# A store at the end of a mixture-of-experts kernel: expert 5's rows divided over two queues

## The chip, the cores and the metric

The kernel runs on one core of a Trainium2 chip. The metric is the device time of one execution in microseconds (us); lower is better. A profile of one execution stands beside the times; its span runs from the first to the last instruction and is a little shorter than the execution's time.

## The reference

Eight experts, each with its own 256 rows of x, its own two weight matrices and biases; everything is float32.

```python
n_experts, capacity, hidden, expert_hidden = 8, 256, 512, 2048

def reference(x, w1, w2, b1, b2):
    h = np.matmul(x, w1) + b1[:, np.newaxis, :]
    h = np.maximum(h, 0)
    return (np.matmul(h, w2) + b2[:, np.newaxis, :]).astype(np.float32)
```

x is 8 x 256 x 512, w1 is 8 x 512 x 2048, w2 is 8 x 2048 x 512, and the output is 8 x 256 x 512. The weights are 64 MB in all, and each is used once.

## The kernel before

**Loads.** Nearly everything is moved by DMAs that GpSimd issues, because these turn float32 in memory into fp16 in SBUF on the way. `load_x`, `load_w1` and `load_w2` fetch one expert each: x in 128 partitions of 2 rows, w1 in 128 partitions of 4 rows of the hidden dimension, w2 in 128 partitions of 16 rows. `load_w2_piece` (its DMA is L91) fetches the last expert's w2 in eight pieces: (0, 4), (4, 7), (7, 10) and (10, 12) of the 16 rows with all 512 columns, then (12, 14) and (14, 16) with the first 320 columns, and both again with the other 192. Only the first two experts' x (by SyncE and ScalarE, as float32) and b1 (by ScalarE) take another way in.

**Products.** For each expert `first_product` makes 16 tiles of h (128 x 256), each of four matmuls (L113); ScalarE adds the bias, applies relu and writes fp16 (L120). `second_product` starts each accumulator with a one-row matmul that adds b2 (L163), then adds up 16 matmuls of 128 x 512 for each of two row halves (L175). For expert 7 the accumulators are split by columns, 320 and 192, to follow the pieces of its w2. The outer loop runs 11 stages: stage s makes the first product of expert s (while there is one) and the second product of expert s - 3.

**Stores.** `store` copies the two accumulators out of PSUM, one by VectorE (L138) and one by ScalarE (L139), into one SBUF tile of 128 partitions x 1024 float32. Each partition is one row of 4 KB in the store: two rows of the output that lie next to each other. For experts 0 to 6 it only notes the store in `pending`; the DMA is issued later by `flush` (L132), on GpSimd. Expert 7's stores go out at once: the 320 columns by SyncE (L149), the 192 columns half by SyncE (L142) and half by ScalarE (L143).

**The ring.** All of GpSimd's DMAs from expert 1 on stand in a list written out by hand, `ring`. Each entry has a stage from which it may be issued, and entries are issued strictly in the list's order; `ordered` keeps that order in the program. In the steady part a stage brings x and w1 of the next expert, w2 of the expert three back, and the store of the expert before that. At the end of the list stand the eight pieces of expert 7's w2, with the store of expert 4 after the first piece. The stores of the experts in `LATE`, 5 and 6, stand behind the last piece, in that order:

```python
    for e in LATE:
        ring.append((e + LAG + 1, flush, (e,)))
```

The waits on GpSimd's DMAs come from data, from free buffers, and from completion counts: the DMAs take turns on eight completion semaphores, so each one waits until the DMA eight places before it in GpSimd's order has landed. For expert 5's store the one eight places before is expert 4's store. For expert 6's store it is the piece (4, 7) of expert 7's w2.

SyncE issues only three DMAs: the first expert's x at the start, and expert 7's two stores (L149, L142) at the end.

Of the kernel before, what the change touches and what calls it, by code (L numbers as in the profile page):

```python
# [11 lines left out]
def kernel(  # L12
# [9 lines left out]
    nc = tc.nc  # L22
    fp32 = mybir.dt.float32
    fp16 = mybir.dt.float16
    E, T, H = x.shape
    M = w1.shape[2]
    P = 128
# [3 lines left out]
    HL = 320  # L31
    LAG = 3
    LATE = (5, 6)
    RING = (0, 1, 2, 3, 4) + LATE
    PARTS = {}
    nXF32 = 2

    def ordered(ins):
        return tc.keep_in_program_order(ins)
# [89 lines left out]

    def flush(e):  # L130
        dst, src = pending.pop(e)
        ordered(nc.gpsimd.dma_start(out=dst, in_=src))  # L132

    def store(e, po, c0, c1, split):
        w = c1 - c0
        pool = out_pool if w == H else singles
        out_sb = pool.tile([P, nTB, w], fp32, tag=f"out{c0}_{w}", name=f"out{w}")
        nc.vector.tensor_copy(out=out_sb[:, 0, :], in_=po[0])  # L138
        nc.scalar.copy(out=out_sb[:, 1, :], in_=po[1])  # L139
        dst = out[e].rearrange("(p tb) h -> p tb h", tb=nTB)[:, :, c0:c1]  # L140
        if split and c1 == H:
            nc.sync.dma_start(out=dst[:, 0, :], in_=out_sb[:, 0, :])  # L142
            nc.scalar.dma_start(out=dst[:, 1, :], in_=out_sb[:, 1, :])  # L143
        elif e in RING:
            pending[e] = (dst, out_sb)
        else:
            step = P // PARTS.get(e, 1)
            for lo in range(0, P, step):
                nc.sync.dma_start(out=dst[lo : lo + step], in_=out_sb[lo : lo + step])  # L149

    def second_product(e):
        if e < E - 1:
# [17 lines left out]
        for lo, hi, p0, p1, t in w2_sb[e]:  # L170
            mine = [b for b in blocks if p0 <= b[0] and b[1] <= p1]
            for tb in range(nTB):
                for j in range(lo, hi):
                    for c0, c1, _, _ in mine:
                        ordered(nc.tensor.matmul(  # L175
                            out=acc[c0, tb],
                            lhsT=hT[e][:, j, tb * P : (tb + 1) * P],
                            rhs=t[:, j - lo, c0 - p0 : c1 - p0],
                            start=False,
                            stop=(j == nJ - 1),  # L180
                        ))
            if hi == nJ:
                for c0, c1, _, _ in mine:
                    store(e, [acc[c0, tb] for tb in range(nTB)], c0, c1, e == E - 1)

    x32 = singles.tile([P, nXF32, nTB, H], fp32)
    for e in range(nXF32):
# [4 lines left out]
        out=b2_sb,  # L192
        in_=b2.rearrange("e h -> (e h)").rearrange("(o f) -> o f", o=1),
# [10 lines left out]
    for j in range(nJ):  # L204
        for s in range(2):
            ordered(nc.tensor.matmul(  # L206
                out=pb[s * 64 : (s + 1) * 64, j, :, :],
# [5 lines left out]
    for s in range(2):  # L213
        nc.vector.tensor_copy(  # L214
            out=b1T[s * 64 : (s + 1) * 64, :, :], in_=pb[s * 64 : (s + 1) * 64, :, :, s]
# [6 lines left out]
    for s in range(1, E + LAG - 1):  # L222
        if s < E:
            if s >= nXF32:
                ring.append((s - 2, load_x, (s,)))
            ring.append((s - 2, load_w1, (s,)))
        if s >= LAG:
            ring.append((s - 2, load_w2, (s - LAG,)))
        if s >= 2 * LAG:
            ring.append((s - 2, flush, (s - 2 * LAG,)))  # L230
    e = E - LAG - 1
    for piece in (
        (0, 4, 0, H), (4, 7, 0, H), (7, 10, 0, H), (10, 12, 0, H),
        (12, 14, 0, HL), (14, 16, 0, HL), (12, 14, HL, H), (14, 16, HL, H),
    ):
        ring.append((0, load_w2_piece, (E - 1,) + piece))
        if e in RING and e not in LATE:
            ring.append((e + LAG + 1, flush, (e,)))
            e += 1
    for e in LATE:  # L240
        ring.append((e + LAG + 1, flush, (e,)))
# [40 lines left out]
```

## Time and profile before

| what | value |
|---|---|
| time, median of 4 runs | 183.57 us (183.33 to 183.68) |
| time of the profiled execution | 183.33 us |
| its span | 181.6 us |
| PE busy | 138.1 us (76% of the span) |
| ScalarE busy | 62.7 us (35%) |
| GpSimd busy | 22.1 us (12%) |
| VectorE busy | 13.4 us (7%) |
| time of GpSimd's DMA packets, share of 16 engines | 97.9% |
| read from and written to memory | 71.39 MB and 4.19 MB |

PE is the name of TensorE's matmuls, PEld of its weight loads, DVE of VectorE, ACT of ScalarE, POOL of GpSimd and SP of SyncE. The sixteen DMA engines serve the queues of GpSimd (q0), SyncE (q1), ScalarE (q10) and the fetches of instructions (q8, q14). Busy time is summed for each engine; the engines run beside each other. A DMA that an engine issues shows as a short instruction on that engine's line, and the time from issue to landing is listed apart; a DMA posts one completion count from each of the sixteen engines, and has landed with the last of them. Line numbers (L132) are those of the kernel before.

### The profile page before, as it was taken

What the parts mean: (1) busy time and instruction counts of PE and PEld (TensorE: products, weight loads), DVE (VectorE), ACT (ScalarE), POOL (GpSimd) and SP (SyncE); (2) the same over time, 40 slices, a digit from 0 to 9 for tenths busy, and PEclk for the clock granted to TensorE, in tenths of its full rate; (3) what the DMA queues carried; (4) which work ended last, traced back from release to release, by engine and by line L of the source; (5) the groups of instructions that cost most, each with busy time, mean ns of one, the idle gap of its engine ahead of it and who ended that gap; (6) DMA issues with size and microseconds to landing.
All of it is one profiled execution on the core that took longest, in us unless ns stands there. A gap on an engine that the chain in (4) does not pass through costs nothing.

```text
span 181.6 us, 2204 instructions
## 1 busy us (share of the span) xinstructions
PE 138.1 (76%) x946; PEld 98.4 (54%) x946; DVE 13.4 (7%) x22; ACT 62.7 (35%) x138; POOL 22.1 (12%) x46
## 2 busy tenths in 40 slices
PE   0555999489640999649995999409999995999990
PEld 0544889369540946547464747308559641334670
DVE  0320011001000101010000110001010010100010
ACT  0022679548560422705136604503309501010100
POOL 7100020300300011010110002000004003113300
PEclk9999999969995699965999999965999999699999
DMA  5989998999999999999999999999999999999995
GB/s 186 283 180 233 231 220 184 209 253 213 193 231 231 206 199 231 198 236 202 231 227 184 224 231 224 184 285 213 199 224 222 280 199 273 211 245 281 215 283 186
DMA packets 7017, 40.58 MB, mean 224 GB/s; under 512 B 1216, under 2 KB 2256, under 8 KB 4960
## 3 DMA queue, kind: packets, MB, share of 16 engines
q0 software_dynamic: 5872, 38.81, 97.9%
q1 hardware_dynamic: 688, 0.95, 1.6%
q10 hardware_dynamic: 448, 0.69, 1.0%
q8 instruction: 7, 0.11, 0.2%
q14 instruction: 2, 0.02, 0.0%
HBM read 71.39 MB, written 4.19 MB: 416 GB/s over the span
## 4 chain that ended last, share of the span: by engine, by line
DMA 60%; PE 25%; issue 8%; another core or an unknown queue 2%; POOL 2%; ACT 0%; POOLq 0%
DMA x<-in_x_dram 24%; DMA w2sb<-in_w_dram 23%; PE acc L175 17%; DMA w1sb<-in_w_dram 13%; PE ph L113 7%; PE acc L163 1%; PE psx L100 1%; POOL w2sb L85 1%; POOL w1sb L75 1%; POOL out_dram L132 0%; POOL b_sb L191 0%; POOL ident masks.py:199 0%; POOL ident masks.py:197 0%; ACT out L139 0%
## 5 line engine op out<-in xcount | busy, mean ns | idle before, releaser
L113 PE MATMUL ph<-xT,w1sb 128*128 128x256 f16 x512 | 67.8, 299 | 8.7 <-DMA w1sb<-in_w_dram 8.7
L120 ACT ACTIVATE hT<-ph,b1T 128x256 f16<-128x256 f32 x128 | 56.9, 474 | 43.6 <-PE ph L113 43.5
L113 PEld LDWEIGHTS <-w1sb 128*128 128x128 f16 x512 | 61.4, 149 | 14.4 <-DMA w1sb<-in_w_dram 9.6
L175 PE MATMUL acc<-w2sb,hT 128*128 128x512 f16 x224 | 51.2, 388 | 2.1 <-DMA w2sb<-in_w_dram 2.1
L175 PEld LDWEIGHTS <-hT 128*128 128x128 f16 x288 | 27.5, 99 | 32.8 <-issue 7.4
L139 ACT COPY out<-acc 128x512 f32<-128x512 f32 (+2 forms) x9 | 4.9, 541 | 60.0 <-PE acc L175 60.0
L100 PE MATMUL psx<-ident,x 128*128 128x128 f16 x64 | 6.6, 265 | 21.5 <-DMA x<-in_x_dram 20.8
L100 PEld LDWEIGHTS <-x 128*128 128x128 f16 x64 | 5.3, 128 | 22.5 <-DMA x<-in_x_dram 21.7
L75 POOL DMA_DIRECT2D w1sb<-in_w_dram x8 | 4.4, 553 | 61.7 <-PE ph L113 60.9
L106 DVE COPY xT<-psx 128x1024 f16<-128x1024 f16 x8 | 5.5, 692 | 83.0 <-PE psx L100 83.0
L138 DVE COPY out<-acc 128x512 f32<-128x512 f32 (+2 forms) x9 | 5.7, 632 | 72.1 <-PE acc L175 72.1
L85 POOL DMA_DIRECT2D w2sb<-in_w_dram x8 | 4.3, 536 | 48.9 <-PE acc L175 48.9
L206 PE MATMUL pb<-ident,b_rows 16*64 16x16 f32 x64 | 3.7, 265 | 6.7 <-DMA b_rows<-in_b_dram 6.7
L175 PE MATMUL acc<-w,hT 128*128 128x320 f16 (+1 forms) x64 | 7.4, 272 | 0.0
L206 PEld LDWEIGHTS pb<-ident,b_rows 16*64 16x64 f32 x64 | 3.6, 198 | 6.7 <-issue 6.7
L91 POOL DMA_DIRECT2D w<-in_w_dram x8 | 5.0, 621 | 12.4 <-DMA w2sb<-in_w_dram 9.4
L132 POOL DMA_DIRECT2D out_dram<-out x7 | 3.8, 542 | 20.5 <-ACT out L139 14.4
L120 ACT ACT_TABLE_LOAD x1 | 1.3, 1283 | 11.2 <-DVE b1T L214 11.2
L163 PE MATMUL acc<-b_sb,ones 1*128 1x512 f16 (+2 forms) x18 | 4.8, 355 | 0.0
L69 POOL DMA_DIRECT2D x<-in_x_dram x6 | 3.3, 545 | 6.2 <-DMA w2sb<-in_w_dram 5.7
L163 PEld LDWEIGHTS <-ones 1*128 1x128 f16 x18 | 1.1, 92 | 2.2 <-issue 2.1
L201 DVE CAST x<-x 128x1024 f16<-128x1024 f32 x2 | 1.4, 694 | 4.4 <-DMA x<-in_x_dram 4.3
(9 smaller groups left out, 2.6 us busy)
## 6 DMA issues: line engine op xcount, KB each, us to landing
w1sb<-in_w_dram POOLq DMA_DIRECT2D x8, 2048.0 KB, 33.6
w2sb<-in_w_dram POOLq DMA_DIRECT2D x6, 2048.0 KB, 45.8
out_dram<-out POOLq DMA_DIRECT2D x7, 512.0 KB, 28.3
w2sb<-in_w_dram POOLq DMA_DIRECT2D x2, 1024.0 KB, 25.1
x<-in_x_dram POOLq DMA_DIRECT2D x6, 256.0 KB, 38.9
w<-in_w_dram POOLq DMA_DIRECT2D x2, 384.0 KB, 19.2
x<-in_x_dram ACTq DMA_DIRECT2D x1, 512.0 KB, 5.3
x<-in_x_dram SPq DMA_DIRECT2D x1, 512.0 KB, 4.5
```

The lines of the kernel that those rows point to most:

```text
L75: ordered(nc.gpsimd.dma_start(out=w1_sb[e], in_=w1[e].rearrange("(p kc) m -> p kc m", kc=nKC)))
L85: ordered(nc.gpsimd.dma_start(out=t[:, lo : lo + step, :], in_=src[:, lo : lo + step, :]))
L91: ordered(nc.gpsimd.dma_start(out=t, in_=src[:, lo:hi, c0:c1]))
L100: ordered(nc.tensor.transpose(out=pt[:, kc, tb * P : (tb + 1) * P], in_=x16[e][:, tb, :].rearrange("p (q kc) -> p q kc", kc=nKC)[:, :, kc] ...
L106: nc.vector.tensor_copy(out=xT[e], in_=pt)
L113: ordered(nc.tensor.matmul(out=ph, lhsT=w1_sb[e][:, kc, :].rearrange("p (q j) -> p q j", j=nJ)[:, :, j], rhs=xT[e][:, kc, :], start=(kc == 0),
L120: nc.scalar.activation(out=hT[e][:, j, :], in_=ph, func=mybir.ActivationFunctionType.Relu, bias=b1T[:, j, e : e + 1], scale=1.0,)
L138: nc.vector.tensor_copy(out=out_sb[:, 0, :], in_=po[0])
L139: nc.scalar.copy(out=out_sb[:, 1, :], in_=po[1])
L163: ordered(nc.tensor.matmul(out=t, lhsT=ones1, rhs=b2_sb[0:1, e * H + c0 : e * H + c1], start=True, stop=False,))
L175: ordered(nc.tensor.matmul(out=acc[c0, tb], lhsT=hT[e][:, j, tb * P : (tb + 1) * P], rhs=t[:, j - lo, c0 - p0 : c1 - p0], start=False, sto ...
L206: ordered(nc.tensor.matmul(out=pb[s * 64 : (s + 1) * 64, j, :, :], lhsT=b1_rows.rearrange("r (q j) -> r q j", j=nJ)[:, :, j], rhs=ident[0 ...
```

## The change

The store of expert 5 is divided by partitions. Partitions 0 to 24 (25 rows of 4 KB) are stored by SyncE as soon as expert 5's result is in SBUF. Partitions 25 to 120 (96 rows) and 121 to 127 (7 rows) stay in GpSimd's ring, as two DMAs in place of one, in the same place behind the last piece of expert 7's w2. The change was given with the words "25 rows by SyncE (five DMA engines), the other rows in the ring in parts of 96 and 7".

The lists `RING` and the old `PARTS` go away. What they decided, namely that experts 0 to 6 go through the ring and expert 7 does not, is now decided by `split` and `e < E - 1`, with the same outcome.

```diff
     LATE = (5, 6)
-    RING = (0, 1, 2, 3, 4) + LATE
-    PARTS = {}
+    PARTS = {e: ((0, 25, True), (25, 121, False), (121, 128, False)) for e in (5,)}
...
     def flush(e):
         dst, src = pending.pop(e)
-        ordered(nc.gpsimd.dma_start(out=dst, in_=src))
+        for p0, p1, sync in PARTS.get(e, ((0, P, False),)):
+            if not sync:
+                ordered(nc.gpsimd.dma_start(out=dst[p0:p1], in_=src[p0:p1]))
...
         if split and c1 == H:
             nc.sync.dma_start(out=dst[:, 0, :], in_=out_sb[:, 0, :])
             nc.scalar.dma_start(out=dst[:, 1, :], in_=out_sb[:, 1, :])
-        elif e in RING:
+        elif split:
+            nc.sync.dma_start(out=dst, in_=out_sb)
+        else:
+            for p0, p1, sync in PARTS.get(e, ()):
+                if sync:
+                    nc.sync.dma_start(out=dst[p0:p1], in_=out_sb[p0:p1])
             pending[e] = (dst, out_sb)
-        else:
-            step = P // PARTS.get(e, 1)
-            for lo in range(0, P, step):
-                nc.sync.dma_start(out=dst[lo : lo + step], in_=out_sb[lo : lo + step])
...
-        if e in RING and e not in LATE:
+        if e not in LATE and e < E - 1:
             ring.append((e + LAG + 1, flush, (e,)))
             e += 1
```

In the order of instructions, SyncE gets one DMA more (25 x 1024, between the first x and expert 7's stores), GpSimd one more (96 x 1024 and 7 x 1024 in place of 128 x 1024), and the other engines' instructions stand as before. With one DMA more in GpSimd's order, the turn of the eight completion semaphores shifts by one behind it: the 7 rows wait for the piece (4, 7), and expert 6's store for the piece (7, 10).

## The prediction

> **What bounds the kernel now.** I read the page first (sixteen DMA engines, and the chain that ended last), then busy time by stage over the last 30 us, then the timelines of the two engines whose queues the change touches, then the landings.
>
> The page's DMA row and chain say that this kernel is a stream of transfers: nine tenths or more in nearly every slice, and DMA the largest share of the chain.
>
> ```profile
> DMA  5989998999999999999999999999999999999995
> DMA 60%; PE 25%; issue 8%; another core or an unknown queue 2%; POOL 2%; ACT 0%; POOLq 0%
> ```
>
> By stage (PE busy comes second, the DMA share second from the right) the last 20 us look like this. The engines are full until 179.2 and nearly full to the end, while PE has half a microsecond left after the last load.
>
> ```profile
> core 0: us, PE busy (x) PEld busy (x) DVE busy (x) ACT busy (x) POOL busy (x), PEclk, DMA share, GB/s
> 160.00:169.00 9.00, 9.00 (x43) 3.75 (x40) 0.69 (x1) 0.59 (x1) 2.12 (x4) 1.00 1.02 266
> 169.00:176.60 7.60, 7.60 (x66) 5.74 (x65) 0.49 (x1) 0.82 (x2) 1.10 (x2) 1.00 1.21 240
> 176.60:179.20 2.60, 0.53 (x5) 0.26 (x3) 0.36 (x1) 0.51 (x2) 0.00 (x0) 1.00 0.85 327
> 179.20:181.60 2.40, 0.00 (x0) 0.00 (x0) 0.00 (x0) 0.00 (x0) 0.00 (x0) 0.92 0.23 74
> ```
>
> The timelines of GpSimd and SyncE: the last load (L91) is issued at 167.96; the stores of experts 5 and 6 (L132) follow; SyncE idles until expert 7's stores (L149, L142).
>
> ```profile
> 167.96 0.71 POOL L91 DMA_DIRECT2D w<-in_w_dram  x1 [1.56 <-DMA w<-in_w_dram]
> 169.96 0.55 POOL L132 DMA_DIRECT2D out_dram<-out  x1 [1.29 <-ACT out L139]
> 171.42 0.55 POOL L132 DMA_DIRECT2D out_dram<-out  x1 [0.91 <-DMA w<-in_w_dram]
> ...
> 176.82 0.62 SPq L149 DMA_DIRECT2D out_dram<-out  x1
> 177.49 0.59 SPq L142 DMA_DIRECT2D out_dram<-out  x1
> ```
>
> From issue to landing: the shortest of line L91, the shortest of L132, and SyncE's last store.
>
> ```profile
> DMA to landing us min/median/max: 8.6/17.2/30.0
> ...
> DMA to landing us min/median/max: 7.7/28.3/49.0
> ...
> out_dram<-out SPq DMA_DIRECT2D x1, 96.0 KB, 3.0
> ```
>
> So the last load lands at 167.96 + 8.6 = 176.6, expert 6's store at 171.42 + 7.7 = 179.1, SyncE's last store at 177.49 + 3.0 = 180.5; 1.0 us of closing waits ends the span of 181.6, and the execution took 183.33 (1.7 outside the span).
>
> These are the last of sixteen counts each, one for each DMA engine, and the trace's completion records hold them singly. For the last load: 175.07 to 176.60, nine engines within the first 0.42 us and seven from 0.91 to 1.53 us behind the first. Expert 5's store: 176.35 to 177.92. Expert 6's: 177.59 to 179.17. SyncE's last: thirteen from 180.00 to 180.16, then 180.39, 180.44, 180.53. The seven laggards stem from seven 16 KB packets of the instruction queue (21 to 163 us), each setting one engine back by about 1 us for good. **The end is set by three lagging engines, and there by the length of their queue**: the slowest starts its last row of expert 6 at 178.65, and its packets for expert 7 then end at 180.18, 1.37 us after that row; 16 of 0.052 us and 16 of 0.033 us make 1.36, so this engine doesn't wait for anything.
>
> **The change, part by part.**
>
> *Price of a row.* A store of 128 rows is 8 rows of 4 KB on each engine; between the last counts of the two stores lie 179.17 − 177.92 = 1.25 us, or 0.155 us a row.
>
> *Removed and put in the ring.* Expert 5's store becomes 96 rows (6 on each engine) and 7 rows (one on each of seven engines). A lagging engine gets 6 rows, or 7, in place of 8: 0.31 us less, or 0.155 less. It is all on the path that sets the end, because that engine is busy without a gap to 180.18. What is late next: engines on time, whose last counts come at 180.00 to 180.16 because expert 7's stores are issued no earlier. 180.53 − 0.31 = 180.22 stays above that, so the whole 0.31 counts; the floor is 180.53 − 180.00 = 0.53 at most.
>
> *Added on SyncE.* 25 rows on five engines (the number is the change's own) are 5 rows each, 5 × 0.155 = 0.78 us on each of the five. SyncE waits for both copies of expert 5, done at 162.40, and issues in 0.6 us (as L149 and L142): free at 163.0. Behind it is only L149 at 176.82, so the added wait delays nothing. The 0.78 us falls before or among the last loads. An engine less than 1.53 − 0.78 = 0.75 us behind the first hides it: its last load still lands before the slowest engine's. Over the whole tail such an engine carries 5 + 6 + 1 = 12 rows at most where it had 8, 0.62 us more, so its ring runs to about 177.6 + 0.6 = 178.2, just where expert 7's packets begin (178.08). Cost zero to 0.1 us there, and not at the end. For an engine that lags, see the first rival. The trace has no transfer on fewer than sixteen engines, and does not number the engines. Bounds for the cost of this part: nothing, if all five are on time; +0.62 us, if the slowest is among the five and gets one of the 7 rows. I take nothing.
>
> The reason is weak but from the trace: packet records of one queue that start in the same nanosecond stand in a fixed order, and where they belong to different transfers of the last 8 us, the engine that is ahead stands first in 66 of 76 such ties. So engines ahead are mostly those listed first, and a transfer with five engines, if it takes those at the low end of the list, would meet them.
>
> The Trainium skill ("DMA: Bandwidth & Descriptors", section "Why a DMA increments its semaphore by 16 and not by 1") says that a transfer issued by SyncE or ScalarE runs on the largest number of engines up to 16 that divides its rows, and on the lowest-numbered of them. No run here shows it; by it, 25 rows meet engines 0 to 4.
>
> *GpSimd's queue.* One more DMA, 0.55 us by L132's rows, in a stretch in which GpSimd is busy 1.1 of 7.6 us. Every GpSimd DMA here waits for the one eight places before it. The 7 rows wait for the load that landed at 170.81, which expert 6's store waited for; that store now waits for the next one, landed at 172.63, and goes out at about 173.2 in place of 171.42. Nothing is queued behind it. The work that hides this is the ring: loads to 175.1 on the first engine and expert 5's rows after them to about 176.3, 3 us after the issue. If that cover were gone (the first ring load of the kernel took from 1.26 to 5.17 to start), engines on time would idle 0.8 us, which they have. Cost: nothing. The DMA of 96 rows keeps the old one's place at 169.96.
>
> *All else* (the renamed branch for expert 7, flushes 0 to 4, PE, ScalarE, VectorE) is the same instructions in the same order. One more wait among SyncE's closing waits is 0.06 us if it stands last, which the rows at 178 to 180.6 hide.
>
> *Sum.* 183.33 − 0.31 = 183.02 for the profiled execution. That lies 0.24 below the median of the four runs, so against the median 183.57 I forecast 183.26.
>
> A rule speaks against the change. The DMA share of 1.00 from 160 to 179 says that there is no idle engine to win. The skill's same page ("Rules for kernel authors") says that spreading transfers over SyncE, ScalarE and GpSimd does not add bandwidth, as all share the same sixteen engines. By it alone the sum would be zero: 183.57. The completion counts differ from it, since the sixteen don't end together: 1.53 us lie between first and last.
>
> **Rivals.**
>
> *One of the five lags (slower).* Place: SyncE's 5 rows stand in a lagging engine's queue, which is then 5 + 6 − 8 = 3 rows longer, +0.47 us, or +0.62 with one of the 7. It decides from an engine that is over 1.58 − 0.47 = 1.11 us behind (five of the seven are). Also the last load lands up to 0.78 later, and PE and expert 7's stores with it: 180.00 + 0.78 = 180.78, less than 180.53 + 0.47 = 181.00, so the queue decides. Time: 184.04, to 184.19. For it: seven of sixteen lag, and five drawn at random would seldom miss them. Against it: the ties. Chance 0.20.
>
> *Nothing moves.* The 7 rows fall on the lagging engines, or the end hangs on the issue of expert 7's stores (SyncE's two, one after the other from 176.82 to 178.08) more than on the queue. Then −0.1 to +0.1, 183.5 to 183.7. Against it: thirteen engines are done 0.37 us before the end. Chance 0.10.
>
> *The forecast.* Five engines on time, laggards relieved by one or two rows: −0.15 to −0.5, own range 183.05 to 183.45. Chance 0.70.
>
> **How the numbers follow.** 0.2% is 0.37 us, about what a measurement of this kernel can tell from no change. The forecast's 0.31 lies just inside it; with the runs' spread of 0.35 us I give 0.33 of its 0.70 to faster by over 0.2% and 0.37 to within. The slower rival gives 0.19 to slower and 0.01 to within; the last 0.07 to within and 0.03 to slower. Faster 0.33, within 0.45, slower 0.22. Range 182.95 to 184.0: from the floor of 0.53 and 0.1 for the runs, up to the lagging-engine case, of which the dearer half is left out.
>
> **What would show it.** Right: a SyncE store at about 162.4; the last load's counts still end near 176.6; expert 5's and 6's last counts 0.15 to 0.31 earlier; SyncE's last count near 180.2. Wrong: the last load's counts end after 176.8, and PE's last matmul with them (rival one); SyncE's last count unmoved with expert 6's earlier (rival two); any row before 162 that moved.

## The result

| | median | runs |
|---|---|---|
| before | 183.57 us | 59 (183.19 to 184.49) |
| changed | 183.33 us | 37 (182.91 to 184.12) |

The ratio is 0.9987, with a 95% interval of 0.998 to 0.9993: a gain of 0.24 us, between 0.13 and 0.37. The interval lies below 1, and the gain is within the 0.2% (0.37 us) that the prediction took for no change. The same pair, run once more later, gave 0.9993 (0.9981 to 1.0005): 0.13 us, with an interval that includes no gain.

The profiled execution of the changed kernel is the slowest of its 37, at 184.12 us, so its absolute times can't be laid beside those of before. The first lines are from its page, in the order of those of before: the span, the DMA row and the chain.

```profile
span 182.3 us, 2208 instructions
DMA  5999999999999999999999999999999999999994
DMA 60%; PE 25%; issue 8%; another core or an unknown queue 3%; POOL 2%; ACT 0%; POOLq 0%
```

By stage, cut at its own last load (177.66) and at expert 6's store (179.91); the last three columns are the granted clock, the DMA share and GB/s:

```profile
core 0: us, PE busy (x) PEld busy (x) DVE busy (x) ACT busy (x) POOL busy (x), PEclk, DMA share, GB/s
160.00:169.00 9.00, 9.00 (x42) 3.81 (x41) 0.42 (x2) 0.58 (x1) 2.13 (x3) 1.00 1.02 270
169.00:177.66 8.66, 8.66 (x70) 6.13 (x69) 0.81 (x2) 0.88 (x2) 2.33 (x4) 1.00 1.18 244
177.66:179.91 2.25, 0.52 (x5) 0.26 (x3) 0.36 (x1) 0.45 (x2) 0.00 (x0) 1.00 0.63 237
179.91:182.30 2.39, 0.00 (x0) 0.00 (x0) 0.00 (x0) 0.00 (x0) 0.00 (x0) 0.76 0.32 101
```

By the counts, the stretch from the last load to expert 6's store took 2.57 us before (176.60 to 179.17; the table of before cuts at 179.20) and takes 2.25 now, 0.32 less; from there to the end it is 2.4 in both. The DMA share in it fell from 0.85 to 0.63: fewer rows follow the last load, and this execution's engines end further apart.

The timelines of GpSimd and SyncE (L136 is `flush`, L153 the new store, L149 and L146 expert 7's):

```profile
169.01 0.71 POOL L93 DMA_DIRECT2D w<-in_w_dram  x1 [1.69 <-DMA w<-in_w_dram]
170.99 0.54 POOL L136 DMA_DIRECT2D out_dram<-out  x1 [1.28 <-ACT out L143]
172.09 0.54 POOL L136 DMA_DIRECT2D out_dram<-out  x1 [0.56 <-DMA w<-in_w_dram]
174.29 0.55 POOL L136 DMA_DIRECT2D out_dram<-out  x1 [1.66 <-DMA w<-in_w_dram]
...
163.41 0.36 SPq L153 DMA_DIRECT2D out_dram<-out  x1
177.81 0.61 SPq L149 DMA_DIRECT2D out_dram<-out  x1
178.48 0.59 SPq L146 DMA_DIRECT2D out_dram<-out  x1
```

and the landings: the shortest of the loads (L93), the shortest of the ring's stores (L136), SyncE's last store.

```profile
DMA to landing us min/median/max: 8.7/17.3/30.5
...
DMA to landing us min/median/max: 5.6/23.4/50.1
...
out_dram<-out SPq DMA_DIRECT2D x1, 96.0 KB, 2.8
```

Last load at 169.01 + 8.7 = 177.7; expert 6's store, for which GpSimd waited 1.66 us (a load, by the shifted order of the completion semaphores), at 174.29 + 5.6 = 179.9; SyncE's last store at 178.48 + 2.8 = 181.3. From the last load's last count to SyncE's last count (called the tail below) the completion records give 181.27 − 177.66 = 3.61 us, against 180.53 − 176.60 = 3.93 before. **The tail is 0.32 us shorter; two rows at 0.155 are 0.31.**

Why did this execution take longer in spite of it? The last load's first count came at 175.19, as before (175.07), but its last came 2.47 us behind, not 1.53. Four engines got their first packet of GpSimd's queue at 6.09 to 6.23 us, the others at 5.13 to 5.40 (before: all at 5.17 to 5.43), and stood 0.99 to 1.10 us behind the first on the first load. By 157.7 us, before any of SyncE's 25 rows had moved, the slowest engine was 2.44 us behind (before: 1.45). So the last load came 1.06 us later, and with the tail 0.32 shorter and 0.04 more closing waits that is 0.78 of the 0.79 us between 184.12 and 183.33. A second profile of the changed kernel, of an execution of 182.97 us, has a lag of 1.31, the last load at 176.46 and a tail of 3.63.

### The profile page after: what moved, and what is told of

It is laid out like the page before. It is cut to its first block, busy times and chain, and to the rows that moved or that the text cites. A ratio compares the mean times of both kernels' runs of the same rounds, so it can differ in the third digit from the quotient of the medians.

```text
span 182.3 us, 2208 instructions
## 1 busy us (share of the span) xinstructions
PE 136.9 (75%) x946; PEld 97.7 (54%) x946; DVE 13.3 (7%) x22; ACT 62.6 (34%) x138; POOL 22.7 (12%) x47
## 4 chain that ended last, share of the span: by engine, by line
DMA 60%; PE 25%; issue 8%; another core or an unknown queue 3%; POOL 2%; ACT 0%; POOLq 0%
DMA x<-in_x_dram 24%; DMA w2sb<-in_w_dram 23%; PE acc L180 16%; DMA w1sb<-in_w_dram 13%; PE ph L115 7%; PE acc L168 1%; PE psx L102 1%; POOL w2sb L87 1%; POOL w1sb L77 1%; POOL out_dram L136 0%; POOL b_sb L196 0%; POOL ident masks.py:199 0%; POOL ident masks.py:197 0%; ACT out L143 0%
## 5 line engine op out<-in xcount | busy, mean ns | idle before, releaser
L115 PE MATMUL ph<-xT,w1sb 128*128 128x256 f16 x512 | 66.7, 295 | 8.4 <-DMA w1sb<-in_w_dram 8.3
L115 PEld LDWEIGHTS <-w1sb 128*128 128x128 f16 x512 | 60.7, 148 | 13.7 <-DMA w1sb<-in_w_dram 9.4
L136 POOL DMA_DIRECT2D out_dram<-out x8 | 4.3, 540 | 22.6 <-ACT out L143 14.4
L93 POOL DMA_DIRECT2D w<-in_w_dram x8 | 5.0, 624 | 12.9 <-DMA w2sb<-in_w_dram 9.9
```

What stands on the lines that cost most here:

```text
L93: ordered(nc.gpsimd.dma_start(out=t, in_=src[:, lo:hi, c0:c1]))
L115: ordered(nc.tensor.matmul(out=ph, lhsT=w1_sb[e][:, kc, :].rearrange("p (q j) -> p q j", j=nJ)[:, :, j], rhs=xT[e][:, kc, :], start=(kc == 0),
```

## The experiments

The theory: the engine that lags most sets both ends, the landing of the last load and the end of the tail. Rows taken out of its queue behind the last load shorten the tail; rows put before the last load cost nothing on engines that are on time. The rivals: rows taken from behind the last load are won whichever engine carries them (one); the division itself or the shifted semaphores bring the gain (two); the end hangs on the issue of expert 7's stores (three).

The completion records of one profile of each kernel, and the ratios to the kernel before from runs on the same chip. "Rows" are those of expert 5's store that a lagging engine has behind its last load; "first" is the first engine's count of the last load, "lag" how far behind the last one is.

| stores | rows | first, us | lag, us | tail, us | ratio (95%) |
|---|---|---|---|---|---|
| before | 8 | 175.07 | 1.53 | 3.93 | 1 |
| changed | 6 or 7 | 175.19 | 2.47 | 3.61 | 0.9987 (0.998 to 0.9993) |
| changed, again | 6 or 7 | 175.14 | 1.31 | 3.63 | 0.9993 (0.9981 to 1.0005) |
| 32 by SyncE, 96 in the ring | 6 | 175.54 | 2.16 | 3.62 | 1.0005 (0.9996 to 1.0013) |
| 96 and 32 in the ring | 8 | 175.20 | 1.63 | 3.94 | 1.0003 (0.9995 to 1.0012) |
| 128 by SyncE | 0 | 176.36 | 1.73 | 3.49 | 1.0045 (1.0032 to 1.0057) |
| left out | 0 | 175.26 | 1.82 | 3.62 | 0.9976 (0.9967 to 0.9985) |
| before, with extra loads | 8 | 174.99 | 2.17 | 3.87 | 1.0018 (1.0008 to 1.0028) |
| changed, with extra loads | 6 or 7 | 174.96 | 2.97 | 3.74 | 1.0068 (1.0055 to 1.0082) |
| experts 5 and 6 divided | 6 or 7 of each | 175.19 | 1.99 | 3.58 | 1.0006 (0.9998 to 1.0014) |
| 25 and 7 by SyncE, 96 in the ring | 6 | 175.14 | 1.69 | 3.62 | 0.9979 (0.997 to 0.9988) |
| the same, again | 6 | 175.21 | 1.96 | 3.62 | 0.9986 (0.9977 to 0.9995) |
| changed, 7 rows left out | 6 | 175.21 | 1.86 | 3.61 | 0.9992 (0.9983 to 1.0001) |

**32 rows on all engines.**

```diff
-    PARTS = {e: ((0, 25, True), (25, 121, False), (121, 128, False)) for e in (5,)}
+    PARTS = {5: ((0, 32, True), (32, 128, False))}
```

> 32 rows by SyncE, which all sixteen engines share (2 each), and 96 in the ring. Theory (the engine that lags most decides): that engine carries 8 rows again, 2 of them before its last loads. Last load 0.31 us later, the tail (last load's last count to SyncE's last count, 3.93 us in the profile of before) 0.31 shorter, time unchanged at 183.6, within 0.15. Rival one (rows taken out from behind the last load are won, whichever engine carries them): 2 rows of 0.155 won, 183.25.

Measured 183.58, before 183.5. The tail (3.62) is as short as the changed kernel's, but the first count of the last load is 0.3 to 0.6 us later than in all kernels whose early rows go to five engines or none. What was won behind the last load was lost ahead of it. Rival one is out.

**The division alone.**

```diff
+    PARTS = {5: ((0, 96, False), (96, 128, False))}
```

> Expert 5's store in two parts of 96 and 32 rows, both in the ring, nothing by SyncE; each engine carries 8 rows as before. Theory: no change, 183.6, tail 3.9 us. Rival two (the gain comes from the division itself, or from expert 6's store waiting one place later): 183.3, as the changed kernel.

Measured 183.57, tail 3.94. Expert 6's store waits one place later here too. Rival two is out.

**All rows early.**

```diff
+    PARTS = {5: ((0, 128, True),)}
```

> All 128 rows of expert 5's store by SyncE as soon as they are ready, none in the ring. Theory: every engine carries 8 rows before its last loads, so the last load lands 8 x 0.155 = 1.24 us later, and the tail shrinks only to its floor, by about 0.5 us: 183.57 + 0.7 = 184.3. Rival one: the tail's 0.53 won and nothing lost, 183.05.

Measured 184.29 against 183.5: 0.8 us lost, where the theory said 0.7. All engines' loads are later: the first count of the last load by 1.29 us, and PE now waits for its pieces, as its timeline of the last product shows (the bracket is idle time before the group and what ended it). The first line is the kernel before, where this product ran in one stretch without a bracket; the other two are this run.

```profile
169.75 7.38 PE L175 MATMUL acc<-w,hT 128*128 128x320 f16 x64
...
172.20 1.47 PE L180 MATMUL acc<-w,hT 128*128 128x320 f16 x12 [0.76 <-DMA w<-in_w_dram]
174.06 4.56 PE L180 MATMUL acc<-w,hT 128*128 128x320 f16 x36 [0.39 <-DMA w<-in_w_dram]
```

Rival one is out here as well, by 1.2 us.

**How much there is to win.**

```diff
+    PARTS = {5: ()}
```

> Expert 5's store is left out altogether (its 256 output rows are not written). It shows the most that relief of the ring's end can bring. Theory: the slowest engine's queue is 1.24 us shorter, but the issue of expert 7's stores then decides: 0.4 to 0.55 us won, 183.0 to 183.2, SyncE's last counts within 0.2 us of each other. Rival three (the end hangs on the issue of expert 7's stores already): 0 to 0.1 won, 183.5.

Measured 183.13, before 183.5: 0.44 us won (0.28 to 0.61), with SyncE's last sixteen counts within 0.17 us. With no row of expert 5 left, the tail is 3.62 us, no shorter than with six. The tail gives 0.31 of the 0.44; the interval holds 0.31, and whether anything else was won stays open. From 177.07 (last load) the DMA share was 0.16 until expert 6's store had landed:

```profile
177.07:178.36 1.29, 0.54 (x5) 0.26 (x3) 0.36 (x1) 0.52 (x2) 0.00 (x0) 1.00 0.16 64
```

Here the engines wait for expert 7's result and its issue: rival three is true at about 3.6 us, and false at 3.93. (The 3.49 with all rows early has another start: there SyncE issued expert 7's first store 0.08 us behind the last load, here 0.22.) By the tail, the change takes all that relief of the ring's end can give (0.32 of 0.31); by the time it takes 0.24 of 0.44, with intervals that overlap.

**The five engines made to lag.** At the start SyncE loads 25 rows twice, in a run with the old store (`PARTS = {}`) and in one with the changed store:

```diff
+    extra = singles.tile([25, nTB * H], fp32)
+    for i in range(2):
+        nc.sync.dma_start(
+            out=extra, in_=x[E - 1 - i].rearrange("(p tb) h -> p (tb h)", tb=nTB)[0:25]
+        )
```

> The stores as in the kernel before, but at the start SyncE also loads 25 rows of 4 KB twice into a tile that nothing reads: the five engines of a 25-row transfer then stand 2 x 0.78 = 1.56 us further back for the rest of the kernel. It is the ground for the next run. Theory: the five become the laggards, 1.6 to 2.0 us behind the first in place of 1.53; last load 0.1 to 0.5 us later, 183.6 to 184.0. Rival one (how the rows are spread over engines doesn't matter): the 200 KB are 0.5 us of sixteen engines, 184.0.

Measured 183.90 (before: 183.59), lag 2.17: five engines stand 1.83 to 2.17 us behind the first, the other eleven 0 to 1.34. Both theory (183.6 to 184.0) and rival (184.0) allow the time, but the records show five engines behind, not sixteen.

> The changed kernel with the same two extra loads: now the 25 rows fall on engines that lag. Theory (and the forecast's first rival): their last load lands 0.78 us later than in the run with the extra loads and the old store, their tail shrinks to its floor of 3.5, so the time is 0.4 to 0.5 us above that run: the change turns from a gain to a loss. Rival one: 0.24 below that run, as without the extra loads.

Measured 184.84, 0.94 above the run before it. The sign is as expected, the size double, and rival one (0.24 below) is out. In the records the last load is 0.77 us later (177.93, 177.16): five engines stand 2.56 to 2.97 behind, the other eleven at most 1.54. The tail lost only 0.13, one row, because the five, now the laggards, got one of the 7 each: from their counts of the 96 rows to those of expert 6's store it is 1.41 to 1.46 us, and 1.25 on the slowest engine of the run that leaves the 7 rows out. I had let the tail shrink to its floor. And the stretch from the last count to the end of the span grew from 1.03 to 1.35: the nine transfers of SyncE and ScalarE share eight completion semaphores, the last store took over the first one, and that one stands second among SyncE's closing waits, so seven more waits of 0.06 us ran after it instead of before. 0.77 − 0.13 + 0.32 = 0.96. Without that side effect the 25 rows on lagging engines cost about 0.6 us (0.94 − 0.32), the forecast's first rival at its price of 0.47 to 0.62.

**Expert 6's store as well.**

```diff
+    PARTS = {e: ((0, 25, True), (25, 121, False), (121, 128, False)) for e in (5, 6)}
```

> The division of expert 5's store (25 rows by SyncE, 96 and 7 in the ring) made for expert 6's store as well. Theory: engines not among the five carry 12 to 14 rows in place of 16, 0.3 to 0.6 us less, more than the floor allows (0.4); but the five take 10 rows by SyncE, 1.56 us, of which the second half lands behind or among the last loads: they stand 1.35 to 1.65 us behind, as the laggards did before. 183.4 to 183.9, no better than the changed kernel. Rival one: 0.4 to 0.5 us won, 183.1.

Measured 183.76, before 183.59; as the theory had it. SyncE issues the second 25 rows at 168.6, and they move from 172.0 to 173.8, ahead of the last pieces' landing. Eleven engines then stand 1.26 us or more behind the first, against six on the load ahead of these rows, and the slowest 1.99 against 1.71; the tail stays at its floor (3.58).

**The 7 rows by SyncE.**

```diff
+    PARTS = {5: ((0, 25, True), (25, 32, True), (32, 128, False))}
```

> The 7 rows go by SyncE too, as a second transfer (25, then 7), and 96 stay in the ring. Theory: every engine that lags has 6 rows in the ring and none of the 7 unless it is among SyncE's seven; one DMA less for GpSimd. As the changed kernel or up to 0.1 us better: 183.2 to 183.35. Rival two (the order of GpSimd's DMAs and expert 6's store one place later matter): the gain shrinks or grows with it by over 0.1.

Measured 183.28, before 183.59: 0.39 us won (0.22 to 0.55). It sends the same 32 rows by SyncE as the first experiment, but in parts of 25 and 7 that only some engines carry, and that is the whole difference between a gain and none. Rival two of this run is open: it is 0.15 us better than the changed kernel by the ratios (0.9979 and 0.9987), whose intervals overlap.

To see whether it beats the changed kernel, both ran once more on one chip, with a third in which the 7 rows are left out (`PARTS = {5: ((0, 25, True), (25, 121, False))}`).

> The changed kernel once more, beside the next two on one chip. Theory: 0.2 to 0.35 us below the kernel before, 183.25 to 183.4; last load to SyncE's last count 3.6 us.

> The kernel with 25 and 7 rows by SyncE and 96 in the ring once more. Both this one and the changed kernel have the tail at its floor of 3.6 us, so theory: no more than 0.1 us apart. If the 7 rows in the ring (an engine that lags may get one, 0.155 us) or the later issue of expert 6's store cost something, this one is 0.1 to 0.2 us ahead.

> The changed kernel without the DMA of 7 rows (these 7 partitions of expert 5's output are not written). It prices that DMA. Theory: within 0.1 us of the changed kernel, since the tail's floor is reached with it or without it. If the 7 rows hit engines that lag: 0.1 to 0.15 us ahead of the changed kernel, level with the one that gives them to SyncE.

Measured 183.35, 183.14 and 183.29, before 183.49. The changed kernel is only 0.14 below the kernel before, less than the 0.2 to 0.35 expected, and its interval (0.9981 to 1.0005) includes no gain. The one with the 7 rows by SyncE is 0.21 below the changed one, where theory allowed 0.1: the order hints at a gain for it, but the intervals overlap, the tails are equal, and leaving the 7 rows out altogether brings only 0.06, as expected. It beats the kernel before in both runs; that it beats the changed one stays open.

## Why the prediction was right

The forecast was 183.26, with 0.45 for a change within 0.2%; measured were 183.33 and a gain of 0.24 (0.13 to 0.37) where 0.31 was forecast. The time alone hardly tells so small a gain from none; the tail does, 0.30 and 0.32 us shorter in the two profiles of the changed kernel.

- **Price of a row and relief of the laggards** (0.31): shown. The tail lost 0.32 and, undivided (the division alone), nothing. The slowest engine has 6 rows and none of the 7: from its count of the 96 rows to that of expert 6's store it is 1.26 us, as without the 7 rows (1.25). It was again without a gap to the end: the last row of expert 6 starts at 179.41, the packets for expert 7 end at 180.94, 1.37 us after that row, as before.
- **Cost of the 25 rows at nothing**: shown. In the changed kernel's profile the slowest engine was 2.45 us behind the first on the load just ahead of these rows (first count 166.27) and 2.44 on the next (169.37), while the engines within 0.56 us of the first went from nine to four: all five were on time. With the extra loads, where they were not, the lag grew from 2.12 (at 157.5) to 2.97. In those two profiles the long instruction packets had set none of the five back, or one would stand a further 1 us behind. The weak sign from the order of packet records pointed right: counted over neighbouring records of different sizes in the last 8 us, the engine that is ahead stands first in 53 of 61 ties in the kernel before, but in 14 of 69 and 5 of 46 where the five were made to lag, so the five are among those listed first. That all five would be on time had rested on this sign alone.
- **Five engines**: SyncE's new store has six count records, one at 163.88, as its issue ended, and five from 168.79 to 169.15. This is what the Trainium skill says ("DMA: Bandwidth & Descriptors", section "Why a DMA increments its semaphore by 16 and not by 1"): the engines in use post one each and the issuer the rest at once. That they are the lowest-numbered stays unseen, as the trace doesn't number the engines.
- **Expert 6's store later, one DMA more on GpSimd**: no cost, by the division alone (1.0003).
- **The floor** was mis-sized. The prediction had 0.53 us as the most there is to win; with the store left out it is 0.44 (0.28 to 0.61) by the time and 0.31 by the tail (3.62 against 3.93). I took it from the first of sixteen counts of SyncE's last store (180.00), though even with the store left out they spread over 0.17. It was luck that two rows are worth just this floor: a third would have won nothing, and the sum would have been too high.
- **The signs to look for** held one trap: "the last load's counts end after 176.8" was to mean a lagging engine among the five. They ended at 177.66, for another reason. The lag differs from execution to execution (1.31 and 2.47 for the same kernel), while its first count (175.14 and 175.19) and its tail (3.63 and 3.61) hardly do. In the second profile, of 182.97 us, the signs are as named: last load 176.46, expert 6's last count 178.75, SyncE's 180.09.
- **A misread column**: the prediction's "DMA share of 1.00 from 160 to 179" is the granted clock, one column to the left. The DMA share there is 1.02, 1.21 and 0.85 (packets that overlap count twice), then 0.23, so the engines were not full until 179.2, nor "nearly full to the end". No term of the sum came from it; that the slowest engine has no gap was read from its packets.
- **The rule against the change**, that spreading transfers over engines' queues wins nothing: true of 32 rows on all sixteen (1.0005), not of 25 and 7 rows, which some engines carry and others don't (0.9979 and 0.9986).

## What to carry to other kernels

When sixteen DMA engines are full, look at the completion counts one by one: in this kernel the slowest engine set the end, and moving work from it to engines that were ahead was worth its own packets' time, down to a floor, while the same bytes moved on all engines were worth nothing and on lagging ones cost 0.6 us. Before tuning such a tail, leave the work out once, to see how little there is to win. Compare single profiles by differences that don't depend on the start of the execution, such as last load to last store.

## What the runs showed of the hardware

- Each 16 KB instruction packet (0.9 to 1.0 us long) set one DMA engine back: in the profile of before, the engines 0.85 us or more behind the first number one after the first packet (at 21.0 us), four after the fourth (89.1) and seven after the seventh (163.0). The lag stays: in the changed kernel's profile the slowest engine was 2.44 us behind at 118.8 us and 2.47 at the last load.
- SyncE's 25 rows, issued at 163.77, began to move only at 166.91, 3.1 us later, and then took turns with the ring's store rows, one each (on one engine at 166.91, 167.22, 167.53, 167.84, 168.15). In all nine profiles in which SyncE stores rows of expert 5, the first packet came 3.0 to 3.2 us after the issue had ended; expert 7's first store, when some engines had run dry, took 0.64 (177.44 to 178.08 before). A short transfer from another queue did not overtake the long one at once.
- Which completion semaphore the last store uses moves the end: 0.3 us in the run with nine transfers by SyncE and ScalarE.
